# Later inverse products for the first head pair and earlier weight splits at the start, in a hybrid decoder layer on one Trainium2 core

## The chip, the cores and the metric

The kernel runs on one core of one Trainium2 chip. It is one program that computes a whole layer. The metric is the time of one execution on the device in microseconds (us); several runs are made and their median is given.

Engine names are those of the profile: PE is TensorE (matmuls and transposes; PEld is its weight load), DVE is VectorE, ACT is ScalarE, POOL is GpSimd, and SP is SyncE, which issues the DMAs. Each engine takes its instructions in its own fixed order; an instruction that waits holds up all behind it on the same engine.

## The reference

One layer on x of 512 positions by 1024 features in float32. It projects the normed x to eleven pieces; two token mixers work on them, a short gated convolution and a gated delta rule with 8 heads of 128; a sigmoid-gated sum of both, a residual add and a gated convolutional FFN follow.

```python
h = rmsnorm(x, norm_mix_g[l])
proj = h @ w_in[l]
bg, cg, xv, q, k, v, z, a, b, ga, gb = jnp.split(proj, pts, axis=-1)
y_a = short_conv_branch(bg, cg, xv, conv_a_w[l]) @ w_a_out[l]
y_b = gdn_branch(q, k, v, z, a, b, gdn_conv_w[l], gdn_A_log[l], gdn_dt_bias[l],
                 gdn_norm_g[l]) @ w_b_out[l]
mix = jax.nn.sigmoid(ga) * y_a + jax.nn.sigmoid(gb) * y_b
x = x + mix @ w_o[l]
h = rmsnorm(x, norm_ffn_g[l])
x = x + conv_ffn(h, w_up[l], ffn_conv_w[l], w_down[l])
```

Inside `gdn_branch` the sequence is cut into chunks. Each chunk needs the solution of a lower triangular system, and the chunks are then scanned in order:

```python
L = jnp.where(strict, jnp.einsum('bnhid,bnhjd->bnhij', k_beta, k) * decay, 0.0)
sol = lax.linalg.triangular_solve(eye + L, rhs, left_side=True, lower=True)
def step(state, inp):
    q_c, k_c, u_c, w_c, A_c, gl = inp
    v_new = u_c - jnp.einsum('bhcd,bhde->bhce', w_c, state)
    o = jnp.einsum('bhcd,bhde->bhce', q_c, state) + jnp.einsum('bhij,bhje->bhie', A_c, v_new)
    state = state * jnp.exp(gl)[..., None] + jnp.einsum('bhcd,bhce->bhde', k_c, v_new)
    return state, o
```

## The kernel before, in words

**Products.** A float32 product is made of three products of rounded operands: every weight and every activation is split into a high part (`wh`, `hT[0]`) and a low part (`wl`, `hT[1]`), and `mm3` (L114) adds low by high, high by low and high by high. The weights come in blocks of 1 MB (`raw`, two buffers, loaded at L133 on SP). A block is split in four quarters: ACT casts to `wh` (L138), DVE subtracts to `wl` (L139). The products of a block with hT are matmuls of 512 columns at L106.

**Jobs.** `run_jobs` (L181) goes through a list of blocks: k, q, v and z of head pair 0, of pair 1, k, q, v of pairs 2 and 3, z of both, then the gates, the convolution branch, the output weights and the FFN. At the start of job i the load of block i+2 is issued, and block i+1 is split while job i's products run.

**The order of the rest.** All other work is written as generators in queues (`backs`, `mids`, `chains`, `evacs`, `splits`, `sums_of`). After every slab, 4 matmuls of 512 columns (`SLAB`), `tick()` (L93) takes each queue one step further. So what is emitted between which products is set by how many bare `yield`s stand in a generator.

**A head pair** (two heads by four pieces of 128 positions, 8 matrices of 128x128) goes through three generators.

- `front(pr)` (L611) is in `chains`. It turns k and q (L608), makes products of k with k and q (L643), U and A from them, and the decay matrices Dm (exponentials on ACT, L525, one pair ahead). It inverts the 16x16 diagonal blocks by a recursion on DVE: U's blocks go through DRAM (`ucd`) to UB, 28 small instructions (L690, L692) make TB. TB goes back through DRAM (`tbd`, stored at L698) to T by four loads (L703) on SP.
- `mid(pr)` (L707) is in `mids`. It first waits `Y_T` = 17 slabs, then builds the whole inverse out of T: a DVE transpose TT (L711), products L718 and L727 of 32x32, L749, L760 and L763, L774, L780, with copies between them on ACT (L737, L753, L765, L767, L775, L781), DVE and POOL (L740). They end in `TTf`, which all pairs share.
- `back(pr)` (L786) is appended to `backs` when `mid` is done. It is the scan of four steps n with two heads: products L803 and L804 with the state, r on DVE (L806), the product L816 with TTf, vn on DVE (L818), products L825 (new state, L830 on DVE) and L836 (output, added on DVE at L840, squared on ACT at L841). At the end a factor `fac` (DVE L846, POOL L847) scales vs (L855), which is turned (L608) and multiplied into yb (L860).

The k job of pair 2 forces `back(0)` to its end (`reach`, L881), and so on for later pairs.

**The start** (L389 to L502). x comes in four tiles of 128 positions. For each, `norm_x(t)` squares it on ACT (L439) and makes the factor rt on DVE and POOL; `scale_x(t)` makes xr on DVE (L450); `turn_x` transposes it on PE (L455); `out_x` writes hT on ACT (L465) and DVE. Products with the first half of the positions (tiles 0 and 1) begin before the second half is there: those for the gates (`ab2`, 32 matmul rows) and those of K's first block. Its four quarters are split by four `ks.step()`, and DVE, ACT and POOL keep the order in which this part is written (`manual_schedule`, L471).

Of the kernel before, what the change touches and what calls it, by code (L numbers as in the profile page):

```python
# [28 lines left out]
Y_V, Y_T, Y_G, Y_N, Y_E, SLAB = 4, 17, 16, 3, 4, 4  # L29
Y_F = (5,4,4,2)  # L30
WARM = 3
WQ = 12


class Task:
# [23 lines left out]
def layer_kernel(ctx, tc, x, norm_mix_g, w_in, w_ab, conv_a_w, gdn_conv_w, gdn_A_log, gdn_dt_bias,  # L59
# [14 lines left out]
    def nm(s):  # L74
        cnt[0] += 1
        return f"{s}{cnt[0]}"
# [46 lines left out]
    class Block:  # L123
# [11 lines left out]
        def part(self, name, src):  # L135
            wh = self.wh[name] = wp.tile([P, *self.quarter], F32R, tag="wh", bufs=WQ, name=nm("wh"))
            wl = self.wl[name] = wp.tile([P, *self.quarter], F32R, tag="wl", bufs=WQ, name=nm("wl"))
            act.copy(out=wh, in_=src)  # L138
            dve.tensor_tensor(out=wl, in0=src, in1=wh.bitcast(F32), op=ALU.subtract)  # L139
# [211 lines left out]
    def ab_split():  # L351
        raw = ab_raw
        act.copy(out=ab2[:, :, 0:16], in_=raw)
        dve.tensor_tensor(out=ab2[:, :, 16:32], in0=raw, in1=ab2[:, :, 0:16].bitcast(F32), op=ALU.subtract)
# [34 lines left out]
    with tc.tile_pool(name="st1", bufs=1) as st1:  # L389
# [44 lines left out]
        def norm_x(t):  # L434
            sq = st1.tile([P, D], F32, tag="sq", bufs=2, name=nm("sq"))
            parts = halves[:1] if t > 1 else halves[1:]
            for i, sl in enumerate(parts):
                acc = sst[:, 2 * t + i:2 * t + i + 1]
                act.activation(out=sq[:, sl], in_=xts[t][:, sl], func=AF.Square, accum_out=acc)  # L439
                if i:  # L440
                    dve.scalar_tensor_tensor(out=rt[:, t:t + 1], in0=acc, scalar=1.0 / D, in1=rt[:, t:t + 1],
                                             op0=ALU.mult, op1=ALU.add)
                else:
                    dve.tensor_scalar(rt[:, t:t + 1], acc, 1.0 / D, EPS, op0=ALU.mult, op1=ALU.add)
            pool.tensor_tensor(out=rt[:, t:t + 1], in0=rt[:, t:t + 1], in1=nhalf[:, 0:1], op=ALU.pow)

        def scale_x(t):
            xr = xrs[t] = st1.tile([P, D], F32, tag="xr", bufs=2, name=nm("xr"))
            for sl in halves[:1] if t > 1 else halves[1:]:
                dve.tensor_scalar(xr[:, sl], xts[t][:, sl], rt[:, t:t + 1], None, op0=ALU.mult)  # L450

        def turn_x(t, bs):
            for k in range(ND):
                c = (k % 2) * HS + (t % 2) * P
                pe.transpose(out=bs[k // 2][:, c:c + P], in_=xrs[t][:, k * P:(k + 1) * P], identity=ident)  # L455

        def out_x(lo, bs):
            for ks in ((0, 2, 4, 6), (1, 3, 5, 7)):
                for lw in range(2):
                    for k in ks:  # L460
                        g = wA[:, 120 + k:121 + k]
                        src = bs[k // 2][:, (k % 2) * HS:(k % 2 + 1) * HS]
                        hh = hT[0][:, k, lo:lo + HS]
                        if lw == 0:
                            act.activation(out=hh, in_=src, func=AF.Copy, scale=g)  # L465
                        else:
                            dve.scalar_tensor_tensor(out=hT[1][:, k, lo:lo + HS], in0=src, scalar=g,
                                                     in1=hh.bitcast(F32), op0=ALU.mult, op1=ALU.subtract)

        bs = [bank() for _ in range(ND // 2)]  # L470
        with tc.manual_schedule(engines={mybir.EngineType.DVE, mybir.EngineType.Activation, mybir.EngineType.Pool}):  # L471
            pe.transpose(out=po[:, 0:P], in_=wr, identity=ident)
            norm_x(0)
            scale_x(0)
            turn_x(0, bs)
            norm_x(1)
            dve.tensor_copy(out=wA, in_=po[:, 0:P])
            scale_x(1)
            turn_x(1, bs)
            ab_split()  # L480
            out_x(0, bs)
            o_ab, o_k = bank(), [bank(), bank()]
            ab_products(o_ab, 0, HS)
            ks = Task(k_block.split())
            norm_x(2)
            ks.step()
            scale_x(2)
            norm_x(3)
            ks.step()
            scale_x(3)  # L490
            ks.finish()
            constants()
            products(o_k[0], k_block.wh, k_block.wl, 0, hT, 0, HS, range(ND))
            bs = [bank() for _ in range(ND // 2)]
            for t in (2, 3):
                turn_x(t, bs)
            out_x(HS, bs)
            products(o_k[1], k_block.wh, k_block.wl, 1, hT, 0, HS, range(ND))
# [206 lines left out]
        mids.append(mtask[pr])  # L705

    def mid(pr, U, um, T, rest):  # L707
        for _ in range(Y_T):
            yield
        TT = tl("TT", 2, (P, 8, 32))  # L710
        dve.transpose(out=flat(TT), in_=flat(T))  # L711
        yield
        yield
        o = bank()
        for f in range(8):
            for q in range(4):
                sl = slice(32 * q, 32 * q + 32)
                pe.matmul(o[sl, 32 * f:32 * f + 32], lhsT=um[sl, f, :], rhs=T[sl, f, :], start=True, stop=True)  # L718
        Y = tl("Y", 2, (P, 8, 32))
        act.copy(out=flat(Y), in_=o[:, 0:256])  # L720
        yield
        yield
        o = bank()
        for f in range(8):
            for q in range(4):
                sl = slice(32 * q, 32 * q + 32)
                pe.matmul(o[sl, 32 * f:32 * f + 32], lhsT=TT[sl, f, :], rhs=Y[sl, f, :], start=True, stop=True)  # L727
        T2 = tl("T", 2, (P, 8, 32))
        dve.tensor_tensor(out=flat(T2), in0=flat(T), in1=o[:, 0:256], op=ALU.subtract)
        T = T2  # L730
        TT = tl("TT", 2, (P, 8, 32))
        dve.transpose(out=flat(TT), in_=flat(T))
        reach(pr - 1, SCANNED)
        for q in range(4):
            sl = slice(32 * q, 32 * q + 32)
            if q < 2:
                act.copy(out=T64[sl, :, sl], in_=T[sl])  # L737
        for q in (2, 3, 0, 1):
            sl = slice(32 * q, 32 * q + 32)
            pool.tensor_copy(out=TTf[sl, :, sl], in_=TT[sl])  # L740
        yield
        yield
        s0, s1 = slice(0, 32), slice(32, 64)
        qa = [slice(64 * b, 64 * b + 32) for b in range(2)]
        qb = [slice(64 * b + 32, 64 * b + 64) for b in range(2)]
        o = bank()
        for f in range(8):
            for b in range(2):
                pe.matmul(o[qb[b], 32 * f:32 * f + 32], lhsT=U[qa[b], f, qb[b]], rhs=T[qa[b], f, :],  # L749
                          start=True, stop=True)  # L750
        Y = tl("Y", 2, (P, 8, 32))
        for b in range(2):
            act.copy(out=flat(Y[qb[b]]), in_=o[qb[b], 0:256])  # L753
        yield
        yield
        o1, o2 = bank(), bank()
        for f in range(8):
            fs = slice(32 * f, 32 * f + 32)
            for b in range(2):
                pe.matmul(o1[qa[b], fs], lhsT=Y[qb[b], f, :], rhs=TT[qb[b], f, :], start=True, stop=True)  # L760
        for f in range(8):
            fs = slice(32 * f, 32 * f + 32)
            pe.matmul(o2[s1, fs], lhsT=TT[s1, f, :], rhs=Y[s1, f, :], start=True, stop=True)  # L763
        v32 = lambda a: a.rearrange("p (f c) -> p f c", c=32)
        act.activation(out=T64[s1, :, s0], in_=v32(o2[s1, 0:256]), func=AF.Copy, scale=-1.0)  # L765
        for b in (1, 0):
            act.activation(out=TTf[qa[b], :, qb[b]], in_=v32(o1[qa[b], 0:256]), func=AF.Copy, scale=-1.0)  # L767
        yield
        yield
        Y64 = tl("Y64", 1, (P, 8, 64))  # L770
        lo, hi = slice(0, 64), slice(64, 128)
        o = bank()
        for f in range(8):
            pe.matmul(o[hi, 64 * f:64 * f + 64], lhsT=U[lo, f, hi], rhs=T64[:, f, :], start=True, stop=True)  # L774
        act.copy(out=flat(Y64[hi]), in_=o[hi, :])  # L775
        yield
        yield
        o1 = bank()
        for f in range(8):
            pe.matmul(o1[lo, 64 * f:64 * f + 64], lhsT=Y64[hi, f, :], rhs=TTf[hi, f, hi], start=True, stop=True)  # L780
        act.activation(out=TTf[lo, :, hi], in_=o1[lo, :].rearrange("p (f c) -> p f c", c=64),  # L781
                       func=AF.Copy, scale=-1.0)
        ctask[pr] = Task(back(*rest))
        backs.append(ctask[pr])
# [543 lines left out]
```

## Time and profile before

| | us |
|---|---|
| median of 3 runs | 998.35 |
| lowest, highest run | 998.03, 1000.19 |
| the profiled execution | 1001.66 |
| span of the profile | 1000.0 |
| mean granted TensorE clock in it | 0.99 |
| stretch of pair 0 from the last product ahead of L718 to the end of the inverse, and some products behind it | 94.38 to 126.58 |
| the like stretch of pair 1 | 168.58 to 191.08 |

The span runs from the first to the last instruction of the profiled execution; a little of its time lies outside. In the rows that are quoted below, a row of the timeline gives the start and the length in us, engine, line, operation, tiles written and read, how many instructions of the kind follow one another (x4), and in brackets how long the engine was idle before and what ended that. Matmuls overlap, so starts tell more of PE than ends.

### The profile page before, as it was taken

To read this page: it belongs to the slowest core of one execution; us is meant where nothing else is said; L and a number is where in the kernel's file an instruction comes from. 1 tells how busy PE (TensorE), PEld (TensorE's weight loads), DVE (VectorE), ACT (ScalarE), POOL (GpSimd) and SP (SyncE) were. 2 spreads that over 40 slices of the span, in tenths; PEclk is the share of its full clock that TensorE was granted. 3 is DMA by queue.
4 is the path that set the end of the run, shared out by engine and by line. 5 is a ranking of instruction groups with operands and counts; after the bars stand their busy time and mean duration, and the time that the engine had idled before them with its cause. 6 is when DMAs were issued, how large, how long until landed. Compare 5 with 4: busy or idle time off the path is not lost.

```text
span 1000.0 us, 15801 instructions
## 1 busy us (share of the span) xinstructions
PE 981.1 (98%) x6250; PEld 847.1 (85%) x6250; DVE 677.0 (68%) x1312; ACT 470.4 (47%) x1023; POOL 60.3 (6%) x101
## 2 busy tenths in 40 slices
PE   8998999999999999999999999999999999999997
PEld 5886788887878889999988888998899988888886
DVE  5868378687634867799953552899888888643325
ACT  6785374666434434344742222555454556322313
POOL 3320120202010000000000000000000000000000
PEclk9999799999999999999999999999999999999999
DMA  6443023223121212322432243212323224233202
GB/s 222 144 135 109 27 71 94 75 82 100 53 85 44 85 48 82 124 86 85 169 126 85 91 158 151 104 45 85 126 90 122 85 85 168 85 99 112 85 1 84
DMA packets 33467, 97.71 MB, mean 98 GB/s; under 512 B 19276, under 2 KB 19697, under 8 KB 23025
## 3 DMA queue, kind: packets, MB, share of 16 engines
q1 hardware_dynamic: 33392, 96.70, 28.9%
q8 instruction: 49, 0.80, 0.3%
q14 instruction: 26, 0.20, 0.1%
HBM read 93.27 MB, written 3.42 MB: 97 GB/s over the span
## 4 chain that ended last, share of the span: by engine, by line
PE 95%; DVE 2%; issue 1%; DMA 1%; ACT 1%; SPq 0%; POOL 0%; POOLq 0%; DVEq 0%; ACTq 0%
PE ps L106 86%; PE ps L608 1%; PE ps L643 1%; DMA xt<-in_x_dram 1%; PE ps L816 1%; PE ps L836 1%; DVE cv L304 1%; PE ps L825 1%; PE ps L804 1%; PE ps L803 1%; PE ps L774 0%; PE ps L780 0%; DVE wl L139 0%; PE ps L1150 0%; PE ps L727 0%
## 5 line engine op out<-in xcount | busy, mean ns | idle before, releaser
L138 ACT CAST wh<-raw 128x512 fp32r<-128x512 f32 x378 | 222.2, 618 | 284.7 <-PE ps L106 245.2
L139 DVE TENSOR_TENSOR wl<-raw,wh 128x512 fp32r<-128x512 f32 x378 | 252.2, 687 | 135.3 <-ACT wh L138 134.0
L106 PE MATMUL ps<-hT,wh 128*128 128x512 f32 (+1 forms) x1104 | 320.5, 371 | 1.8 <-ACT wh L138 1.8
L106 PEld LDWEIGHTS ps<-hT,wh 128*128 128x128 f32 x1104 | 198.5, 191 | 30.4 <-ACT wh L138 2.1
L106 PE MATMUL ps<-hT,wl 128*128 128x512 f32 (+1 forms) x552 | 197.6, 367 | 0.9 <-issue 0.5
L106 PE MATMUL ps<-h,wh 128*128 128x512 f32 (+1 forms) x704 | 177.9, 342 | 0.0
L106 PEld LDWEIGHTS ps<-h,wh 128*128 128x128 f32 x704 | 122.6, 190 | 15.0
L106 PEld LDWEIGHTS ps<-hT,wl 128*128 128x128 f32 x552 | 106.2, 192 | 15.8 <-issue 1.3
L106 PE MATMUL ps<-h,wl 128*128 128x512 f32 (+1 forms) x352 | 114.6, 341 | 0.0
L106 PE MATMUL ps<-wh,as 128*128 128x512 f32 x352 | 108.6, 389 | 0.0
L106 PEld LDWEIGHTS ps<-wh,as 128*128 128x128 f32 x352 | 66.1, 188 | 13.6
L106 PEld LDWEIGHTS ps<-h,wl 128*128 128x128 f32 x352 | 66.8, 190 | 7.6
L106 PE MATMUL ps<-wl,as 128*128 128x512 f32 x176 | 68.5, 389 | 0.0
L106 PE MATMUL ps<-ts,wh 128*128 128x256 f32 x320 | 59.2, 283 | 0.0
L304 DVE SCALAR_TENSOR_TENSOR cv<-ps,wA,cv 128x511 f32<-128x511 f32 (+2 forms) x72 | 53.2, 739 | 4.7 <-ACT cv L301 4.4
L106 PEld LDWEIGHTS ps<-ts,wh 128*128 128x128 f32 x320 | 50.6, 192 | 0.0
L159 DVE TENSOR_TENSOR raw<-raw 128x512 f32<-128x512 f32 x72 | 49.4, 686 | 0.9
L106 PE MATMUL ps<-us,wh 128*128 128x256 f32 x256 | 47.4, 283 | 0.0
L106 PEld LDWEIGHTS ps<-us,wh 128*128 128x128 f32 x256 | 40.5, 192 | 0.0
L106 PE MATMUL ps<-wh,mix 128*128 128x512 f32 x128 | 40.2, 391 | 0.0
L106 PE MATMUL ps<-ts,wl 128*128 128x256 f32 x160 | 40.1, 283 | 0.0
L106 PE MATMUL ps<-yb,wh 128*128 128x512 f32 x128 | 39.6, 389 | 0.0
(260 smaller groups left out, 1305.9 us busy)
## 6 DMA issues: line engine op xcount, KB each, us to landing
raw<-in_w_in_dram SPq DMA_DIRECT2D x36, 1024.0 KB, 4.9
raw<-in_w_up_dram SPq DMA_DIRECT2D x22, 1024.0 KB, 4.8
raw<-in_w_down_dram SPq DMA_DIRECT2D x11, 1024.0 KB, 4.9
raw<-in_w_a_out_dram SPq DMA_DIRECT2D x4, 1024.0 KB, 5.0
raw<-in_w_b_out_dram SPq DMA_DIRECT2D x4, 1024.0 KB, 5.0
raw<-in_w_o_dram SPq DMA_DIRECT2D x4, 1024.0 KB, 4.9
Dm<-gtd SPq DMA_DIRECT2D x4, 512.0 KB, 3.9
x<-in_x_dram SPq DMA_DIRECT2D x4, 512.0 KB, 6.4
```

The source lines that it names most:

```text
L106: pe.matmul(o, lhsT=a, rhs=b, start=start, stop=stop, skip_group_check=free)
L138: act.copy(out=wh, in_=src)
L139: dve.tensor_tensor(out=wl, in0=src, in1=wh.bitcast(F32), op=ALU.subtract)
L159: dve.tensor_tensor(out=r[q], in0=a, in1=b, op=op)
L304: dve.scalar_tensor_tensor(out=dst[:, sh:], in0=src[:, :S - sh], scalar=wcol(j), in1=dst[:, sh:], op0=ALU.mult, op1=ALU.add)
L608: pe.transpose(out=o[:, n * P:(n + 1) * P], in_=src[:, n * P:(n + 1) * P], identity=ident)
L643: pe.matmul(o[:, i], lhsT=kqs[:, a, h, 0, sl], rhs=kqs[:, b, h, :, sl], start=a > 0, stop=a + b == 0)
L803: pe.matmul(o[:, 0:P], lhsT=kq[:, h, 0, sl], rhs=St[h], start=True, stop=True)
L804: pe.matmul(o[:, P:2 * P], lhsT=kq[:, h, 1, sl], rhs=St[h], start=True, stop=True)
L816: pe.matmul(o[:, 0:P], lhsT=TTf[:, f, :], rhs=rs[h], start=True, stop=True)
L825: pe.matmul(o2[:, 0:P], lhsT=kn[:, f, :], rhs=vns[h], start=True, stop=True)
L836: pe.matmul(o[:, 0:P], lhsT=A[:, f, :], rhs=vns[h], start=True, stop=True)
```

## The change

Two edits. `mid` of pair 0 waits `Y_T + Y_M` = 27 slabs ahead of its first step where it waited 17; the other pairs wait 17 as before. And in the start the first two `ks.step()`, which split the first two quarters of K's first block, stand ahead of `norm_x(2)`; one stood behind it and one behind `norm_x(3)`. No instruction is added or taken out. All lines behind L32 have a number higher by one in the changed kernel.

```diff
 WQ = 12
+Y_M = 10
@@
             ks = Task(k_block.split())
+            ks.step()
+            ks.step()
             norm_x(2)
-            ks.step()
             scale_x(2)
             norm_x(3)
-            ks.step()
             scale_x(3)
             ks.finish()
@@
     def mid(pr, U, um, T, rest):
-        for _ in range(Y_T):
+        for _ in range(Y_T if pr else Y_T + Y_M):
             yield
```

ACT at the start, where `sq` is the square of a tile of x (L439, then L440) and `wh` a cast of a weight quarter. Before:

```order
L465 ACTIVATE hT_80<-ps_152,wA 128x256
L439 ACTIVATE sq_228,sst<-xt_130 128x1024
L138 CAST wh_232<-raw_128 128x512
L439 ACTIVATE sq_238,sst<-xt_132 128x1024
L138 CAST wh_242<-raw_128 128x512
L138 CAST wh_248<-raw_128 128x512
L138 CAST wh_252<-raw_128 128x512
```

In the changed kernel:

```order
L466 ACTIVATE hT_80<-ps_152,wA 128x256
L139 CAST wh_228<-raw_128 128x512
L139 CAST wh_232<-raw_128 128x512
L440 ACTIVATE sq_236,sst<-xt_130 128x1024
L440 ACTIVATE sq_242,sst<-xt_132 128x1024
L139 CAST wh_248<-raw_128 128x512
L139 CAST wh_252<-raw_128 128x512
```

Both casts that PE's first products of K need now stand ahead of the squares of the third and fourth tile. DVE's subtractions move in the same way.

PE at the first inverse product of pair 0 (L718, then L719, which reads T and um). Before:

```order
L106 MATMUL ps_1078<-hT_80,wh_980 128x512 x2
L106 MATMUL ps_1078<-hT_80,wh_972 128x512 x2
L718 MATMUL ps_1105<-T_959,um_779 32x32 x32
L727 MATMUL ps_1148<-Y_1138,TT_1091 32x32 x32
L106 MATMUL ps_1193<-hT_81,wh_1038 128x512
```

In the changed kernel:

```order
L107 MATMUL ps_1186<-hT_80,wl_1059 128x512
L107 MATMUL ps_1186<-hT_81,wh_1058 128x512
L107 MATMUL ps_1186<-hT_80,wl_1059 128x512
L719 MATMUL ps_1204<-T_959,um_779 32x32 x32
L644 MATMUL ps_1243<-kqs_1007 128x256 x6
L107 MATMUL ps_1186<-hT_81,wh_1066 128x512
```

Between the products `ps_1078`, after which L718 stood, and the new place lie 32 matmuls of 512 columns and two groups of four transposes of pair 1's k (L609). L727 no longer follows L718 at once, and pair 1's products of k and q (L643, then L644) stand between the steps of pair 0's inverse.

DVE in the scan of pair 0 (r, vn: L806 and L818, then one higher; sub and TB: the recursion of pair 1). Before:

```order
L806 SCALAR_TENSOR_TENSOR r_1523<-ps_1520,neG,vs_802 128x128
L806 SCALAR_TENSOR_TENSOR r_1529<-ps_1526,neG,vs_802 128x128
L304 SCALAR_TENSOR_TENSOR cv_1508<-ps_1324,wA,cv_1508 128x509
L818 TENSOR_SCALAR vn_1553<-ps_1551,ap_665 128x128
L818 TENSOR_SCALAR vn_1557<-ps_1555,ap_665 128x128
```

In the changed kernel:

```order
L807 SCALAR_TENSOR_TENSOR r_1555<-ps_1552,neG,vs_802 128x128
L691 TENSOR_TENSOR sub_1579<-UB_1365,TB_1366 64x50
L807 SCALAR_TENSOR_TENSOR r_1561<-ps_1558,neG,vs_802 128x128
L693 TENSOR_TENSOR TB_1366<-TB_1366,sub_1579 64x10x5
L691 TENSOR_TENSOR sub_1579<-UB_1365,TB_1366 64x54
L693 TENSOR_TENSOR TB_1366<-TB_1366,sub_1579 64x9x6
L691 TENSOR_TENSOR sub_1579<-UB_1365,TB_1366 64x56
L819 TENSOR_SCALAR vn_1571<-ps_1569,ap_665 128x128
L819 TENSOR_SCALAR vn_1575<-ps_1573,ap_665 128x128
```

The recursion of pair 1, which came behind the scan of pair 0, now runs among its steps, since the scan starts ten slabs later and the recursion does not.

## The prediction

> **What bounds the kernel now.** I read first the page's head, its busy times and the slices of the TensorE clock, then the table of waits of PE, then windows over the places that these name.
>
> ```profile
> span 1000.0 us, 15801 instructions
> PE 981.1 (98%) x6250; PEld 847.1 (85%) x6250; DVE 677.0 (68%) x1312; ACT 470.4 (47%) x1023; POOL 60.3 (6%) x101
> PEclk9999799999999999999999999999999999999999
> ...
> PE ps L718 <- DMA T<-tbd: 3.6, 4, 2.7
> PE ps L727 <- DVE TT L711: 2.1, 1, 2.1
> PE ps L106 <- ACT wh L138: 1.8, 1, 1.8
> ```
>
> PE is busy for 98% of the span, so only two things can be won: PE's few waits, and time in which its clock was low. The fifth slice (100 to 125 us) has a clock of 0.7. The three longest waits after the first load (in us: total, times, longest) are those that the change touches. In the windows below (start:end, length, busy time of PE, PEld, DVE, ACT, POOL, granted clock, DMA share, GB/s) both stand out again.
>
> ```profile
> 10.46:13.87 3.41, 2.71 (x14) 1.38 (x14) 2.43 (x7) 2.00 (x6) 0.00 (x0) 1.00 0.71 205
> 13.87:17.28 3.41, 1.64 (x11) 1.44 (x12) 2.01 (x5) 3.41 (x8) 1.05 (x3) 1.00 0.68 283
> 17.28:20.70 3.42, 3.42 (x18) 3.42 (x17) 2.21 (x4) 0.57 (x2) 2.99 (x11) 0.50 0.13 17
> 94.38:126.58 32.20, 25.97 (x323) 20.63 (x324) 14.32 (x33) 13.40 (x42) 3.22 (x5) 0.79 0.13 38
> 168.58:191.08 22.50, 22.50 (x332) 18.62 (x332) 14.47 (x33) 14.24 (x43) 3.71 (x5) 1.00 0.15 49
> 99.20:112.86 13.66, 11.01 (x164) 7.82 (x153) 1.91 (x4) 2.76 (x7) 1.57 (x4) 0.50 0.17 69
> ```
>
> A low clock comes in steps of 3.4 us: 3.42 us after a window in which PE was idle for 3.41 - 1.64 = 1.77 us, and 13.66 = 4 x 3.415 us after the waits at L718 and L727. An idle of 3.41 - 2.71 = 0.70 us (first row) cut nothing: the next window ran at 1.00. One such window costs 3.42 x (1 - 0.5) = 1.7 us if PE has work for it.
>
> The Trainium skill (TensorE: Matmul & The Clock Gate, Part 1: The HAM clock gate) says that the clock halves after an idle window of about 3.4 us, 3413 ns on a free-running counter. The length agrees with the rows. That the window must be idle does not: PE worked for 1.64 us of the one that cut. The measurement decides; what the page's rule would make of the new waits is the first rival.
>
> **Removed: the stall at the first inverse.**
>
> ```profile
> 92.40 1.98 PE L106 MATMUL ps<-hT,wh 128*128 128x512 f32 x8
> 95.18 1.78 SPq L703 DMA_DIRECT2D T<-tbd  x4
> 98.61 0.69 PE L718 MATMUL ps<-T,um 32*32 32x32 f32 x58 [0.24 <-DMA T<-tbd]
> ...
> 157.61 2.20 PE L106 MATMUL ps<-hT,wh 128*128 128x512 f32 x9
> 159.65 0.39 PE L106 MATMUL ps<-hT,wl 128*128 128x512 f32 x1
> ```
>
> In the timeline (start, us, engine, line, operation) PE runs out at 92.40 + 1.98 = 94.38. The four loads of T are issued only at 95.18; the last T is there at 98.61. In the order of the change the first L718 stands behind 32 more products of 512 columns, each (159.65 - 157.61) / 9 = 0.227 us: 7.3 us. PE comes to it at 94.38 + 7.3 = 101.7, without counting two groups of transposes, and T has been there for 3 us; TT (L711) too, on a DVE that is less than half busy there. So both waits go, and with them the four low windows.
>
> What that is worth I take from pair 1, whose same stretch runs from L718 to the end of its inverse without a wait: 22.50 us at clock 1.00. It has the eight 512-column products more that the change of place put there (8 x 0.227 = 1.8), so pair 0's stretch would be 20.7 in its place, and the loss is 32.2 - 20.7 = **11.5 us**. As a check: waits 3.6 + 2.1 + four windows of 1.7 = 12.5. I keep 11.5, bounds 10.5 to 12.5.
>
> **Moved: the splits of K's first weights.**
>
> ```profile
> 4.31 0.43 SPq L133 DMA_DIRECT2D raw<-in_w_in_dram  x1
> raw<-in_w_in_dram SPq DMA_DIRECT2D x1, 1024.0 KB, 7.8
> ...
> 9.16 3.02 ACT L465 ACTIVATE hT<-ps,wA 128x256 fp32r<-128x256 f32 x8 [1.48 <-PE ps L455]
> 13.59 1.06 ACT L439 ACTIVATE sq<-xt 128x1024 f32<-128x1024 f32 x1 [1.41 <-DMA xt<-in_x_dram]
> 14.64 0.60 ACT L138 CAST wh<-raw 128x512 fp32r<-128x512 f32 x1
> 15.15 1.05 ACT L439 ACTIVATE sq<-xt 128x1024 f32<-128x1024 f32 x1
> 17.45 0.75 DVE L450 TENSOR_SCALAR xr<-xt,rt 128x1024 f32<-128x1024 f32 x1
> 9.69 3.79 PE L106 MATMUL ps<-hT,ab 128*32 128x256 f32 x16
> 15.30 0.38 PE L106 MATMUL ps<-hT,wh 128*128 128x256 f32 x1 [1.82 <-ACT wh L138]
> 25.13 2.02 PE L106 MATMUL ps<-hT,ab 128*32 128x256 f32 x16
> 26.98 0.28 PE L106 MATMUL ps<-hT,wh 128*128 128x256 f32 x1
> ```
>
> ACT is free at 9.16 + 3.02 = 12.18 and waits to 13.59 for tile 3 of x, with the cast behind it in its queue. The raw weights landed at 4.31 + 7.8 = 12.1. So two casts of 0.60 fit into ACT's wait (12.2 to 13.4), and PE, free at 9.69 + 3.79 = 13.48, goes on at once: 1.82 us won. The idle of the window 13.87 to 17.28 falls under the 0.70 that cut nothing, so its 1.7 us of low clock goes too. Late next is the fourth tile. Its square now starts at 13.59 + 1.06 and its xr is done some 3.05 us behind that square's start (17.45 + 0.75 - 15.15), at 17.7, about 18 behind the two subtractions now ahead on DVE. PE has till then 24 products of (26.98 - 25.13) / 16 = 0.116 us, 2.8, and eight transposes, 1.0: it runs out at 17.3 and waits 0.7. Start-up: 1.82 + 1.7 - 0.7 = **2.8 us**; bounds 1.1 (one window is cut by the new wait after all) and 3.5 (no new wait).
>
> **Added: waits where pair 0's inverse and scan now stand.** The scan is now emitted among pair 1's turn, L643 products and TB recursion. No row shows this mixture; each price is bounded by the nearest rows.
>
> ```profile
> 135.27 0.60 PE L816 MATMUL ps<-r,TTf 128*128 128x128 f32 x4
> 135.69 0.61 DVE L818 TENSOR_SCALAR vn<-ps,ap 128x128 f32<-128x128 f32 x2 [0.58 <-PE ps L816]
> 137.07 0.60 DVE L830 SCALAR_TENSOR_TENSOR S<-S,eGl,ps 128x128 f32<-128x128 f32 x2
> 137.59 0.48 DVE L840 TENSOR_TENSOR vs<-vs,ps 128x128 f32<-128x128 f32 x2
> 139.11 0.80 DVE L806 SCALAR_TENSOR_TENSOR r<-ps,neG,vs 128x128 f32<-128x128 f32 x2 [1.04 <-PE ps L804]
> 140.28 0.61 PE L816 MATMUL ps<-r,TTf 128*128 128x128 f32 x4
> 141.65 0.60 PE L836 MATMUL ps<-vn,A 128*128 128x128 f32 x4
> 145.57 0.29 DVE L855 TENSOR_SCALAR vs<-vs,fac 128x128 f32<-128x128 f32 x1 [1.43 <-POOL fac L847]
> ...
> 150.46 0.21 DVE L690 TENSOR_TENSOR sub<-UB,TB 64x56 f32<-64x56 f32 x1
> 150.70 0.21 DVE L692 TENSOR_TENSOR TB<-TB,sub 64x56 f32<-64x56 f32 x1
> ...
> 206.17 0.60 PE L836 MATMUL ps<-vn,A 128*128 128x128 f32 x4
> 211.49 0.33 PE L608 MATMUL ps<-ident,vs 128*128 128x128 f32 x1 [0.81 <-DVE vs L855]
> ```
>
> Inverse: the copies of T and TTf now share ACT with pair 1's squares and casts. I take 0.3, between nothing (pair 1's inverse has no wait) and the dearest such wait, 2.1.
>
> Scan: a step takes PE 140.28 - 135.27 = 5.0 us. DVE's own part of it is 0.61 + 0.60 + 0.48 + 0.80 = 2.5 us; about twelve recursion steps of 150.70 - 150.46 = 0.24 now stand between, 2.9. That makes 5.4 against 5.0, 0.4 a step over four steps: 1.6. Queued behind a late L818 are L830 and L840 on DVE, and PE's next L825 waits for it. Bounds: nothing, and one recursion pair (0.48) ahead of each of eight handovers, 3.8. The exponentials of pair 2, with the table load ahead of them, now come on ACT in mid-scan; the upper bound holds what they hold up.
>
> Output turn: the first L608 on vs now stands 12 products, 2.7 us, behind the last L836. The way from that L836 to the scaled vs took 145.57 - 141.65 = 3.9 us with DVE nearly clear, and 211.49 - 206.17 = 5.3 in pair 1. I take 5.3, since two subtractions now stand in it as there: 5.3 - 2.7 = 2.6. Bounds: 3.9 - 2.7 = 1.2, and 4.0 with two more instructions of 0.7 ahead.
>
> Clock: an idle of 2.6 us is more than the 1.77 that cut, so one window, 1.7. Bounds: nothing, and two windows, 3.4.
>
> Added together 0.3 + 1.6 + 2.6 + 1.7 = **6.2 us**, between 1.2 and 13.3.
>
> At nothing I cost SP's loads (the round trip of T and the raw blocks change places, each with microseconds to spare) and POOL's (6% busy).
>
> **The sum.** 11.5 + 2.8 - 6.2 = 8.1 us less. The profiled execution took 1001.66 us, span 1000.0, so it would take 993.5. It lies 3.3 us above the median of 998.35. Some of that may be a longer stall at L718 in this one execution, which I cannot see in the others; I count half of it, 1.65, as not to be won there. Beside the median the change then wins 11.5 + 2.8 - 1.65 = 12.65 and pays 6.2: 998.35 - 12.65 + 6.2 = 991.9, so **992 us**. On this change alone 988.5 to 996.
>
> **The rivals.**
>
> *The clock holds through the new waits.* If only a window with hardly any work cuts, the wait of 2.6 us, spread over two windows or beside 0.8 us of work in one, leaves the clock at 1.00. For it: the window with 0.70 us of idle. Against it: the one with 1.77 and 1.64 of work. It gives 1.7 less, 990.2. The Trainium skill (TensorE: Matmul & The Clock Gate, Part 1: The HAM clock gate) has this rule.
>
> *The new waits are hidden.* Pair 1's own scan, beside pair 2's front, has one wait of 0.8 us in this trace. Then about 1.5 of the 6.2 comes: 998.35 - 12.65 + 1.5 = 987.2. Against it: the recursion of the next pair and the twelve products are not what pair 1 has.
>
> *The stall is only moved.* The waits come near their upper bounds, 2.1 + 3.8 + 4.0 and two windows of 1.7, 13.3 in all: 998.35 - 12.65 + 13.3 = 999.0. Against it: it needs every handover late.
>
> *Slower: a low clock across the scan.* If PE idles for over 1.8 us early in the scan, the clock drops there; at half clock each link of the scan takes longer, and the idles between keep it low, as they did for four windows behind L718. Held over four steps and the turn, some 23 us, that is seven windows, 7 x 1.7 = 11.9, with the waits of 0.3 + 1.6 + 2.6 = 4.5 it is 16.4: 998.35 - 12.65 + 16.4 = 1002.1. From six windows on it is slower by more than can be told from no change. Against it: a slow PE waits less for the others, and four windows in a row stood behind 3.6 + 2.1 = 5.7 us of waits at once.
>
> *The change does not do what it says.* T still missing at L718 is shut out by 3 us. That the raw weights land behind the third tile would lose the 2.8 us: 994.7; they are issued ahead of it and landed 1.5 us earlier.
>
> **How the numbers follow.** The forecast 0.56, the clock holding 0.15, hidden waits 0.12, only moved 0.08, slower 0.06, weights late 0.03. The range for 8 in 10 cuts off a little at the hidden waits and takes in most of the forecast's worse half: 987 to 997. What a measurement of this kernel can tell from no change is about 0.2%, 2.0 us. Faster by more (under 996.35) are all of the clock holding, the hidden waits and late weights, and 0.52 of the forecast: 0.82. Within it: the forecast's other 0.04 and 0.06 of the moved stall, 0.10. Slower: 0.08.
>
> **What would show it.** In the changed kernel's trace: no wait at the first L719 and clock 1.00 from 94 to 113; no wait at L107 near 13.5 and 1.00 from 17.3 to 20.7; waits of 1.2 to 4 us at the L609 on vs of pair 0, with one low window behind; small waits at L817 or L826. A low clock for over six windows in the scan, or a wait for T again, would make the prediction wrong.

## The result, and the profile after

| | before | changed |
|---|---|---|
| median of 4 runs, us | 998.19 | 988.01 |
| lowest, highest | 995.16, 1000.19 | 987.75, 989.34 |
| span of the profiled execution | 1000.0 | 986.0 |

The ratio is 0.9903 with a 95% interval of 0.9876 to 0.993: 10 us or 1% faster. The forecast was 992 in a range of 987 to 997. The time lies in the range, but below the forecast's own 988.5 to 996, next to the second rival (the new waits are hidden, 987.2).

The head of the changed kernel's page, and the longest waits of PE (us in total, times, longest):

```profile
span 986.0 us, 15803 instructions
PE 974.4 (99%) x6250; PEld 841.9 (85%) x6250; DVE 677.1 (69%) x1312; ACT 470.3 (48%) x1023; POOL 60.6 (6%) x101
PEclk9999999999999999999999999999999999999999
...
PE ps L609 <- DVE vs L856: 2.0, 3, 0.8
PE ps L430 <- DVE warm L394: 1.5, 1, 1.5
PE ps L728 <- DVE U L648: 0.5, 1, 0.5
PE ps L456 <- DVE xr L451: 0.4, 1, 0.4
```

The waits for T, for TT and for the first cast of K are gone, and so is the 7 in the clock's row. New is the wait at L609 for the scaled vs; 0.8 of its 2.0 us is pair 1's, which stood before too. The windows of the changed kernel (start:end, length, busy time of PE, PEld, DVE, ACT, POOL, clock, DMA share, GB/s):

```profile
10.46:13.87 3.41, 3.11 (x19) 1.92 (x19) 3.41 (x8) 3.41 (x9) 0.00 (x0) 1.00 0.99 326
13.87:17.28 3.41, 3.41 (x31) 3.20 (x29) 1.87 (x6) 2.42 (x6) 1.90 (x4) 1.00 0.56 228
17.28:20.70 3.42, 3.34 (x27) 3.14 (x28) 3.42 (x8) 2.97 (x9) 2.90 (x12) 1.00 0.30 72
94.00:114.00 20.00, 20.00 (x301) 16.18 (x300) 14.51 (x33) 13.50 (x49) 7.23 (x9) 1.00 0.37 96
139.22:142.63 3.41, 2.25 (x11) 1.45 (x10) 2.89 (x8) 0.17 (x1) 0.49 (x1) 1.00 0.65 269
```

In the start the window that had 1.77 us of idle is full, and from 94 to 114 us PE does not stop. Of these rows only the last, at the output turn, has an idle of note, 1.16 us, and the clock stayed.

To see where the time came from, I counted the products of 512 columns that read hT and a weight (L106, then L107) in the timelines. There are 2880 of them, in the same order in all kernels. The table compares the starts of the 1st, the 240th (the last one ahead of the old place of L718), the 391st (past pair 0's turn) and the last.

| us | before | changed | gain |
|---|---|---|---|
| start to 1st | 33.29 | 29.66 | 3.63 |
| 1st to 240th | 60.70 | 60.71 | 0 |
| 240th to 391st | 66.79 | 56.81 | 9.98 |
| 391st to last | 832.33 | 832.02 | 0.31 |

So all but 0.3 us of the 14 us between the two profiled executions lies in the two places of the change.

### The profile page after: what moved, and what is told of

The parts are those of the page before. It is cut to its first block, busy times and chain, and to the rows that moved or that the text cites. A ratio compares the mean times of both kernels' runs of the same rounds, so it can differ in the third digit from the quotient of the medians.

```text
span 986.0 us, 15803 instructions
## 1 busy us (share of the span) xinstructions
PE 974.4 (99%) x6250; PEld 841.9 (85%) x6250; DVE 677.1 (69%) x1312; ACT 470.3 (48%) x1023; POOL 60.6 (6%) x101
## 3 DMA queue, kind: packets, MB, share of 16 engines
q1 hardware_dynamic: 33392, 96.70, 29.5%
HBM read 93.27 MB, written 3.42 MB: 98 GB/s over the span
## 4 chain that ended last, share of the span: by engine, by line
PE 94%; DVE 2%; ACT 2%; issue 1%; POOL 1%; DMA 0%; SPq 0%; POOLq 0%; DVEq 0%
PE ps L107 86%; PE ps L609 1%; PE ps L644 1%; PE ps L817 1%; PE ps L837 0%; PE ps L826 0%; PE ps L781 0%; PE ps L775 0%; PE ps L805 0%; PE ps L804 0%; DMA xt<-in_x_dram 0%; PE ps L1151 0%; POOL fac L848 0%; DVE wl L140 0%; ACT hT L466 0%
## 5 line engine op out<-in xcount | busy, mean ns | idle before, releaser
L107 PE MATMUL ps<-hT,wh 128*128 128x512 f32 (+1 forms) x1104 | 318.1, 368 | 0.0
L107 PEld LDWEIGHTS ps<-hT,wh 128*128 128x128 f32 x1104 | 196.2, 189 | 27.9
L107 PE MATMUL ps<-hT,wl 128*128 128x512 f32 (+1 forms) x552 | 194.7, 362 | 0.1
L107 PE MATMUL ps<-h,wh 128*128 128x512 f32 (+1 forms) x704 | 177.9, 341 | 0.0
L107 PEld LDWEIGHTS ps<-h,wh 128*128 128x128 f32 x704 | 122.5, 189 | 15.0
L107 PEld LDWEIGHTS ps<-hT,wl 128*128 128x128 f32 x552 | 104.5, 189 | 14.2 <-DVE wl L140 0.5
L107 PE MATMUL ps<-h,wl 128*128 128x512 f32 (+1 forms) x352 | 114.6, 341 | 0.0
L107 PE MATMUL ps<-wh,as 128*128 128x512 f32 x352 | 108.4, 389 | 0.0
L107 PEld LDWEIGHTS ps<-wh,as 128*128 128x128 f32 x352 | 66.1, 188 | 13.7
L107 PEld LDWEIGHTS ps<-h,wl 128*128 128x128 f32 x352 | 66.7, 190 | 7.6
L107 PE MATMUL ps<-wl,as 128*128 128x512 f32 x176 | 68.5, 389 | 0.0
L107 PE MATMUL ps<-ts,wh 128*128 128x256 f32 x320 | 59.2, 283 | 0.0
L305 DVE SCALAR_TENSOR_TENSOR cv<-ps,wA,cv 128x511 f32<-128x511 f32 (+2 forms) x72 | 53.2, 740 | 3.2 <-ACT cv L302 2.9
L107 PEld LDWEIGHTS ps<-ts,wh 128*128 128x128 f32 x320 | 50.6, 192 | 0.0
L107 PE MATMUL ps<-us,wh 128*128 128x256 f32 x256 | 47.4, 283 | 0.0
L107 PEld LDWEIGHTS ps<-us,wh 128*128 128x128 f32 x256 | 40.5, 192 | 0.0
L107 PE MATMUL ps<-ts,wl 128*128 128x256 f32 x160 | 40.1, 283 | 0.0
L107 PE MATMUL ps<-wh,mix 128*128 128x512 f32 x128 | 40.1, 391 | 0.0
L107 PE MATMUL ps<-yas,wh 128*128 128x512 f32 x128 | 39.6, 389 | 0.0
```

The lines of the kernel that those rows point to most:

```text
L107: pe.matmul(o, lhsT=a, rhs=b, start=start, stop=stop, skip_group_check=free)
L305: dve.scalar_tensor_tensor(out=dst[:, sh:], in0=src[:, :S - sh], scalar=wcol(j), in1=dst[:, sh:], op0=ALU.mult, op1=ALU.add)
```

## The experiments

The measure for the second place is the stretch from the 240th to the 391st product. In every kernel PE has the same work in it: 515 matmuls and transposes, equal in number line by line. It is 55.2 us in the three executions in which PE did not wait at all in it (e4, e10, e11 below), so what is over 55.2 is counted here as waits and low clock. The compared kernel is the one before, run on the same chip; its medians there were 996.92 (e1 to e4), 998.26 (e5 to e8) and 997.6 (e9 to e11).

**One part alone.** e1 keeps `Y_M = 0` and moves only the splits; e2 moves only the inverse:

```diff
-Y_M = 10
+Y_M = 0
```

> Only the earlier splits of K's first two quarters; the inverse of pair 0 stands where it stood before. Theory A (the two edits act apart from each other, each in its own stretch): the wait of 2.2 us at the first product of K (1.82 and 0.34 us) and one low clock window (1.7 us) go, so the second gates product starts 3.6 to 3.9 us earlier than in the kernel before (21.3 to 21.5 us in place of 25.1), and the stall at the first inverse product stays, 10 to 12.5 us. Span some 996.3, median 3.5 us under before. Theory B (the start gained 3.6 us in the changed kernel because the third tile of x happened to land 0.7 us earlier in that execution): the fourth tile is waited for by about 0.7 us and the gain is 2.8 to 2.9.

Measured: 994.74 us, ratio 0.9982 (0.9971 to 0.9994). The second gates product started at 21.71 and the 1st wide product at 29.90, 3.4 us earlier than before, and PE did not wait for the fourth tile. That is nearer to theory A, but it does not rule out theory B: in e1, too, the third tile was there early, by 13.13 us, when its square started without a wait. The stall was there, but cheaper than expected: the stretch took 63.82 us, 8.6 over 55.2 where the kernel before had 66.79 - 55.2 = 11.6. The waits and windows of e1:

```profile
PE ps L719 <- DMA T<-tbd: 3.3, 4, 2.6
PE ps L728 <- DVE TT L712: 2.4, 1, 2.4
...
89.14:92.55 3.41, 1.84 (x9) 1.18 (x7) 2.15 (x4) 2.31 (x5) 0.00 (x0) 1.00 0.47 130
92.55:95.96 3.41, 1.34 (x64) 1.02 (x64) 2.83 (x5) 0.90 (x2) 0.00 (x0) 1.00 0.55 96
95.96:99.38 3.42, 1.37 (x65) 1.33 (x66) 1.28 (x3) 1.06 (x3) 0.00 (x0) 0.50 0.62 256
99.38:102.79 3.41, 3.12 (x7) 1.96 (x7) 0.63 (x2) 0.81 (x2) 1.57 (x4) 0.50 0.02 5
102.79:106.20 3.41, 3.41 (x66) 2.40 (x66) 0.00 (x0) 0.73 (x2) 0.00 (x0) 1.00 0.00 0
```

and the windows of the kernel before at the same place:

```profile
95.80:99.22 3.42, 1.26 (x64) 1.02 (x64) 2.98 (x5) 0.91 (x3) 0.00 (x0) 1.00 0.53 86
99.22:102.63 3.41, 1.30 (x73) 1.19 (x66) 1.13 (x3) 1.21 (x3) 0.00 (x0) 0.50 0.66 267
102.63:106.04 3.41, 2.87 (x6) 1.78 (x7) 0.78 (x2) 0.81 (x2) 1.57 (x4) 0.50 0.02 5
106.04:109.46 3.42, 3.42 (x38) 2.42 (x37) 0.00 (x0) 0.73 (x2) 0.00 (x0) 0.50 0.00 0
109.46:112.87 3.41, 3.41 (x46) 2.44 (x45) 0.00 (x0) 0.01 (x1) 0.00 (x0) 0.50 0.00 0
```

The waits add up to the same (5.7 us in both), but two windows ran low in e1 and four before. So the same waits cost 3 us more or less, two windows of 1.7. Why two windows more stayed low in one of the two executions is not shown here; the last two of them had PE at work throughout.

For e2 the first part goes back, against the changed kernel:

```diff
-            ks.step()
-            ks.step()
             norm_x(2)
+            ks.step()
             scale_x(2)
             norm_x(3)
+            ks.step()
             scale_x(3)
```

> Only the later inverse of pair 0; the start is as before. Theory A: the wait at the first product of K (2.2 us) and the low window from 17 to 21 us are there, the stall at the first inverse product (11.5 us) is not, and the output turn of pair 0 waits 1.2 us: 11.5 - 1.2 = 10.3 us less than the profile before, span some 989.7, and clock 1.00 from 92 to 116 us. Theory B (the clock stays full in the stretch of the inverse only because nothing was low earlier, or the new waits are only hidden when everything comes 3.6 us earlier): a low window or waits of over 2 us come back in the scan, and less than 8 us is won.

Measured: 990.42 us, ratio 0.9934 (0.9919 to 0.9949), span 988.9. The stretch took 56.78 us, as in the changed kernel (56.81): in these executions the second place owes nothing to the first. In the start PE waited 1.2 and 0.3 us, less than the expected 2.2, and one window was low. Theory A. Of the medians, e1 wins 2.2 and e2 6.5 us, together 8.7, against 10.0 to 10.2 for both; the kernel before alone varies by 5 us from run to run, so the 1.4 us between are not to be read as an effect.

**Is the scan bounded by DVE?** The changed kernel with the recursion's product made three times:

```diff
-            dve.tensor_tensor(out=t, in0=UB[:, j, j + 1:16]...
+            for _ in range(3 if pr == 1 else 1):
+                dve.tensor_tensor(out=t, in0=UB[:, j, j + 1:16]...
```

> The changed kernel, with the product of each step of pair 1's recursion (L691) made three times in place of once, same result: 28 more instructions of some 0.24 us on DVE, 6.7 us, most of them among the scan of pair 0. Theory A (the scan's hand-overs are covered by the products between them, and DVE has room there): under 1.5 us of new waits on PE. Theory B (the step of the scan is bounded by DVE, 5.4 us of DVE to 5.0 of PE as the prediction reckoned): each of some two and a half steps grows by 2.9 us, 5 to 7 us longer than the changed kernel, span 991 to 993.

Measured: 986.98 us (986.86 to 989.01), span 987.3; the stretch took 56.13 us, no longer than the changed kernel's 56.81. (The profiled execution was the slowest of the four, 989.01; its 1st wide product started at 31.50.) Theory A. The only wait that names the recursion is one of 0.9 us at the turn. A step of the scan in the changed kernel, and then two in e3 (columns as in the windows above):

```profile
124.90:129.91 5.01, 5.01 (x34) 4.49 (x33) 4.49 (x23) 2.42 (x8) 0.00 (x0) 1.00 0.00 0
```

```profile
126.75:131.75 5.00, 5.00 (x33) 4.49 (x32) 4.60 (x22) 2.37 (x8) 0.00 (x0) 1.00 0.00 0
131.75:136.76 5.01, 5.01 (x33) 4.49 (x32) 4.66 (x23) 4.98 (x17) 0.00 (x0) 1.00 0.00 2
```

A step takes 5.0 us with PE never idle, in all three. The tripled recursion does not crowd a step further: in the order of DVE's instructions it spreads over more steps (still running at the turn), with DVE at 4.6 to 4.7 of 5.0 us. So more work on DVE cost the scan nothing, but no step held more than DVE can do in 5.0 us; what such a step would cost is not shown.

**What the turn waits for.** With `Y_M = 8` 20 products stand between pair 0's last L837 and its turn, with 10 there are 12, with 14 there are 11:

```diff
-Y_M = 10
+Y_M = 8
```

> The changed kernel with 8 slabs more in place of 10. The first inverse product stands 24 products of 512 columns (5.5 us and two groups of transposes) behind the old place in place of 32, T was there 4.2 us behind it; the output turn of pair 0 stands 20 products (4.5 us) behind the last L837 in place of 12 (2.7 us). Theory A (the only new wait is the way from L837 to the scaled vs, 3.5 to 3.9 us, against the products that cover it): no wait at T, none or up to 0.3 us at the first turn, span 0.8 to 1.2 us under the changed kernel's, some 985. Theory B (the waits at the turn come from DVE being busy with the convolution of the next k, whatever stands in front): the 1.2 us stay, span 986.

Measured: 986.82 us (986.5 to 987.06), span 985.3. No wait at pair 0's turn; the stretch took 55.22 us, 1.6 less than with 10 slabs. Theory A. A wait of 0.6 us appeared in pair 1's inverse (L728, ACT's copy of Y), which gives some of it back. For 14 slabs:

> The changed kernel with 14 slabs more. The end of pair 0's scan is now forced by the k job of pair 2: 3 products between the last L817 and L837, 11 ahead of the first turn. Theory A (each new wait is the chain's length less the products that cover it): 0.3 to 0.7 us at L837, the turn's waits of 1.2 us grow by up to 0.5, span 986.3 to 987.2. Theory B (my prediction's size, a crowded scan pays several us and a low window): span 990 or more.

Measured: 987.65 us (987.58 to 987.71), span 985.9, stretch 56.62: one wait of 1.13 us at the turn, none at L837. That is far from theory B. Of theory A the waits it asked for did not come: nothing at L837, and the turn waited 1.13 us in place of 1.2 to 1.7.

**How long a wait halves the clock.** Three kernels leave waits of other lengths: 2 slabs and 6 slabs in place of 10, and one split in place of two ahead of the third tile's square.

> The changed kernel with 2 slabs more in place of 10. PE now reaches the bulk of the first inverse products 5 products (1.1 us) behind the old place, T landed 4.2 us behind it, and L728 stands 3 products behind them. Both theories: 2.5 to 3 us of waiting for T, about 1.4 us (2.1 less 0.7) at L728, no wait at the output turn of pair 0, so 2.8 us more waiting than in the changed kernel. Theory A (an idle of about 1.8 us in one window of 3.4 us halves the clock for the next): at least two low windows, 3.4 us more, span 991 to 993. Theory B (only a window with hardly any work halves it): clock 1.00, span 988 to 989.

Measured: 993.46 us, ratio 0.9962 (0.9949 to 0.9974), span 991.5, stretch 61.52: 6.3 over 55.2, of it 2.8 a wait for T and 3.4 two low windows. The expected wait at L728 did not come. The low windows are theory A's; but the window ahead of them had only 0.68 us of work, so that this run alone does not rule out theory B.

> The changed kernel with 6 slabs more. T is there (24 products behind the old place), but L728 stands right behind L719 with nothing between, as in the kernel before; the output turn stands 28 products behind the last L837. Both theories: no wait for T, 2.1 to 2.7 us at L728 (ACT's copy of Y), none at the turn: 1 us more waiting than the changed kernel. Theory A (1.8 us of idle in one window halves the clock): 1.7 us more if the wait falls within one window, span 987 to 989. Theory B: clock 1.00, span 986.5 to 987.2.

Measured: 987.96 us, span 986.0, stretch 56.91, one wait of 1.2 us at L728, clock 1.00. The wait came out at half of what both theories asked for, so it does not tell them apart.

```diff
             ks.step()
-            ks.step()
             norm_x(2)
             scale_x(2)
             norm_x(3)
+            ks.step()
             scale_x(3)
```

> The changed kernel with only the first quarter of K split ahead of the third tile's square; the second again behind the fourth tile's. PE starts the products of K at once, and after eight of them (0.9 us) waits for the second quarter: cast behind both squares, at some 15.9 us with the third tile landing at 13.6 (15.2 with 12.9), so 1 to 1.7 us of wait in place of none. Theory A (over 1.8 us of idle in one window is needed to halve the clock): no low window, the start 0.9 to 1.7 us longer than in the changed kernel, second gates product at 22.4 to 23.2. Theory B (any wait over 1 us halves it): 1.7 us more, 24 to 25.

Measured: 988.85 us (988.27 to 990.8), span 989.1; the profiled execution was the slowest of the four. In it PE waited 2.0 us up to 16.36, more than expected: the third tile's transposes stood next on PE, and their xr was done at 16.21, the second quarter's cast not much later. One window was low; the 1st wide product started at 32.73, 3.1 later than in the changed kernel. With 2.0 us of idle both theories have the low window, so this too leaves the choice open; but with one split ahead most of the start's gain was lost in this execution. One window of each kernel that bears on the question, in the order e5, e6, e8 and e2, each with the window behind it:

```profile
90.77:94.19 3.42, 0.68 (x3) 0.22 (x2) 2.30 (x4) 2.70 (x5) 0.00 (x0) 1.00 0.30 37
94.19:97.60 3.41, 3.38 (x11) 1.82 (x11) 1.97 (x4) 1.25 (x2) 0.00 (x0) 0.50 0.72 188
```

```profile
96.65:100.06 3.41, 2.23 (x118) 1.46 (x118) 2.56 (x5) 2.59 (x11) 0.00 (x0) 1.00 0.61 255
100.06:103.47 3.41, 3.41 (x77) 2.71 (x66) 3.10 (x6) 2.62 (x11) 0.70 (x2) 1.00 0.02 5
```

```profile
13.42:16.83 3.41, 1.41 (x12) 1.23 (x12) 1.37 (x4) 3.24 (x7) 1.02 (x2) 1.00 0.71 286
16.83:20.24 3.41, 3.41 (x19) 3.41 (x18) 2.25 (x4) 0.61 (x2) 2.98 (x11) 0.50 0.18 24
```

```profile
12.38:15.80 3.42, 1.86 (x13) 1.35 (x12) 1.81 (x5) 3.01 (x6) 0.55 (x1) 1.00 0.94 331
15.80:19.21 3.41, 3.41 (x18) 3.41 (x17) 2.75 (x6) 1.25 (x3) 2.96 (x8) 0.50 0.02 7
```

Idle of 2.74, 2.00 and 1.56 us halved the clock of the next window; 1.18 did not, nor 1.57 in e1's window from 89.14, nor 1.42 in that of the kernel before from 92.39. In e2 PE worked for 1.86 us of the window, more than half: that rules out theory B. Between 11 us and the last 20 us of the thirteen profiled executions every window at full clock with an idle of 1.77 us or more was followed by a low one, and none with 1.42 or less. So the border lies between these, near 1.6 us or 45% of a window. Since 1.56 cut and 1.57 did not, the idle time alone, with the modelled ends of matmuls, does not fix it.

**The changed kernel again, and a better one.** e9 is the changed kernel, e10 has 8 slabs, and e11 has 8 slabs and pair 1's inverse three slabs earlier:

```diff
-        for _ in range(Y_T if pr else Y_T + Y_M):
+        for _ in range(Y_T + Y_M if pr == 0 else Y_T - (pr == 1) * 3):
```

> The changed kernel as it is, beside the next two on one chip. Expected: median 987 to 989, output turn of pair 0 with 1.2 us of waits, clock 1.00 from 10 us to the last 6 us.

> 8 slabs in place of 10, once more beside the changed kernel. Theory A (the turn's wait is the way to the scaled vs less the products ahead of it, and 20 products cover it): the stretch from the last product ahead of the old place to 150 products later is 1.2 to 1.6 us shorter than in the changed kernel, median about 1 us lower. Theory B (the gap between e4 and the changed kernel was the start of one execution): same median within 0.5 us and the same stretch.

> 8 slabs for pair 0, and pair 1's inverse three slabs earlier (14 in place of 17), so that pair 1's output turn stands 16 products (3.6 us) behind its last L837 in place of 13. Theory A: the wait of 0.8 us at that turn goes, T of pair 1 is there in time (landed 6 to 7 us ahead), span 0.6 to 1.0 us under that of 8 slabs alone. Theory B (the turn waits for DVE's other work, not for the chain): no difference.

| | median of 5, us | lowest, highest | ratio to before (95%) | stretch |
|---|---|---|---|---|
| e9, 10 slabs | 987.56 | 987.33, 987.65 | 0.9905 (0.9887 to 0.9923) | 56.77 |
| e10, 8 slabs | 986.97 | 986.66, 987.25 | 0.9899 (0.9882 to 0.9917) | 55.25 |
| e11, 8 slabs, pair 1 at 14 | 985.32 | 984.63, 985.81 | 0.9882 (0.9862 to 0.9902) | 55.22 |

e9 came as expected, with 1.17 us of waits at the turn of pair 0. For e10 theory A: the stretch is 1.5 us shorter again, and the median 0.6 lower, since the 0.6 us at pair 1's L728 came again. For e11 theory A: pair 1's wait at the turn is gone, and the one at L728 too, so that more is won than the expected 0.6 to 1.0; a wait of 0.4 us for pair 1's T is new. The view of PE's waits lists only these:

```profile
PE ps L430 <- DVE warm L394: 1.5, 1, 1.5
PE ps L537 <- ACT abT L533: 0.4, 1, 0.4
PE ps L719 <- DMA T<-tbd: 0.4, 1, 0.4
```

e11 beats both kernels: 985.32 against 987.56 and 997.6 on the same chip, and its slowest run is faster than the fastest run of the changed kernel.

## Why the prediction came out as it did

**The stall at the first inverse (11.5 us): right.** The stretch had 66.79 - 55.2 = 11.6 us over a stretch without waits, and T was never waited for at the new place. What the estimate could not see is that this is one execution's price: in e1 it was 8.6. The prediction took half of the profile's 3.3 us over the median off the gain; the size fits the two windows, 3.4 us, by which the two profiled stalls differ. The spread of the kernel before (994.6 to 1000.2 over all its runs, against 987.3 to 989.3 for the changed one) fits this too, for the granted clock of its runs is on record: the 35 runs beside the experiments took 994.6 to 996.1 us where it was 0.995, and 999.8 to 1000.1 where it was 0.990. A difference of 0.005 in some 997 us is 5.0 us. So the spread is time at the low clock; at which place in the kernel it lay is known for the profiled executions only.

**The start (2.8 us): right, but for the new wait's size.** The wait for the cast and the low window went, and with them a wait of 0.34 us at L106 that the sum had left out. The new wait of 0.7 us for the fourth tile did not come in this execution. The rows of the changed kernel show why:

```profile
11.87 1.19 ACT L139 CAST wh<-raw 128x512 fp32r<-128x512 f32 x2
12.90 1.13 ACT L440 ACTIVATE sq<-xt 128x1024 f32<-128x1024 f32 x1
...
16.24 2.10 PE L456 MATMUL ps<-ident,xr 128*128 128x128 f32 x16
21.50 2.02 PE L107 MATMUL ps<-hT,ab 128*32 128x256 f32 x16
```

The third tile was there by 12.90, 0.7 us before it was in the profile before (13.59). Where its square had to wait for it and started later (13.32 in e10, 13.82 in e3), PE did wait for the fourth tile, 0.3 us in both: the mechanism holds, with less than half of the price. Over the profiled executions the 1st wide product started at 30.0 on average with both splits ahead (ten executions, 29.5 to 31.5) and at 32.9 without (two, 32.5 and 33.3): 2.9 us. The arrival of the third tile varies by 1 us among them (12.79 to 13.82 where it was waited for), so that 2.9 lies so near to 2.8 partly by luck.

**The new waits (6.2 us): the step that failed, in size.** Against 55.2 the changed kernel's stretch has 1.6 us. Its parts:

- Inverse, 0.3: no wait.
- Scan, 1.6: no wait. The prediction added twelve recursion steps of 0.24 us to 2.5 us of the scan's own DVE work and got 5.4 of DVE to 5.0 of PE in each of four steps. Two things are wrong in this. The recursion has only 28 instructions, so twelve a step can stand in 2.3 steps and not in four; in the changed kernel they ran from 121.78 to 131.07, not quite two steps. And the measured step has 4.49 although some 15 of them fall into it: with 2.35 us for the scan's own eight instructions that leaves 0.14 us for each. The 0.24 us was the distance of two starts in a chain in which each instruction needs the one before. An instruction that does not need the one ahead of it starts sooner:

```profile
125.24 0.21 DVE L691 TENSOR_TENSOR sub<-UB,TB 64x56 f32<-64x56 f32 x1
125.37 0.59 DVE L819 TENSOR_SCALAR vn<-ps,ap 128x128 f32<-128x128 f32 x2
125.89 0.20 DVE L693 TENSOR_TENSOR TB<-TB,sub 64x56 f32<-64x56 f32 x1
```

The first vn starts 0.13 us behind the recursion's product, not 0.24, and ahead of that product's end. The kernel before showed the same where pair 0's scaling ran among pair 1's recursion: an L690 at 146.66, the L855 behind it at 146.77, 0.11 us later. A sum of distances along a chain bounds the chain, not the engine.

- Output turn, 2.6: measured 1.16 in two waits, at the lower bound of 1.2. The way from L837 to the scaled vs took 3.5 us, nearer to pair 0's own 3.9 before than to pair 1's 5.3, which I chose:

```profile
136.28 0.61 PE L837 MATMUL ps<-vn,A 128*128 128x128 f32 x4
139.74 0.88 DVE L856 TENSOR_SCALAR vs<-vs,fac 128x128 f32<-128x128 f32 x4 [1.76 <-POOL fac L848]
140.17 0.83 PE L609 MATMUL ps<-ident,vs 128*128 128x128 f32 x4 [0.55 <-DVE vs L856]
140.53 0.75 DVE L305 SCALAR_TENSOR_TENSOR cv<-ps,wA,cv 128x511 f32<-128x511 f32 x1
141.19 0.28 DVE L856 TENSOR_SCALAR vs<-vs,fac 128x128 f32<-128x128 f32 x1
141.62 0.30 PE L609 MATMUL ps<-ident,vs 128*128 128x128 f32 x1 [0.61 <-DVE vs L856]
```

  DVE is idle for 1.76 us ahead of the first scaling: POOL's instruction, not DVE's queue, sets this way, and the first wait, 0.55 us, is the way less its cover. The second, 0.61, is another: here DVE's queue sets it, for an instruction of the next k's convolution (L305, 0.75 us) stands between the fourth scaling and the fifth. In e4, with 20 products in place of 12, all eight scalings ran together from 138.59 on (1.66 us), and both waits went:

```profile
140.11 1.03 PE L609 MATMUL ps<-ident,vs 128*128 128x128 f32 x8
```

  Of the stretch's 1.6 us the remaining 0.45 shows as no wait; what it is stays open.
- Clock, 1.7: no low window. It hung on the wait of 2.6; the 1.16 us that came stay under what halved it elsewhere.

So of the rivals the hidden waits came nearest, with 1.6 for its 1.5 us. Its chance of 0.12 looks too low: four small prices were each taken above the lower bound that the nearest quiet row gave, and all four came out at that bound. The first rival (the clock holds through a wait of 2.6 us) cannot be judged by the changed kernel, since that wait did not come. The Trainium skill (TensorE: Matmul & The Clock Gate, Part 1: The HAM clock gate) asks for an idle window to halve the clock. The traces differ: 1.56 us of idle in a window of 3.42 did it (e2), and 2.00 (e8), so its rule would price such waits too low. The stall that only moves and the low clock across the scan did not come, and no run here brought them about.

## What to carry to other kernels

Price a stall by two lines, the wait and the low clock windows behind it, and compare the stretch with a like one that has no wait: the windows doubled the price here (5.7 us of waits, 11.6 in all), and made it differ by 3 us between two executions. When work is moved under cover, count the products that stand between the ends of the chain that was moved: 12 products (2.7 us) against a way of 3.5 left a wait, 20 left none. And do not add up distances of a dependent chain as load on its engine: among other work an instruction of the chain took about 0.14 us of DVE here, not 0.24. Count the instructions first, too; 28 cannot load four steps with twelve each.

## What the runs showed of the hardware that was not expected

The clock was halved after windows in which PE still worked for more than half of the time (1.86 of 3.42 us, e2). The way back is not even either. In the kernel before the window from 106.04 to 109.46 was full and the next was low all the same, and in e5 the one from 94.19 with 3.38 us of work was followed by a second low one. In the starts of the kernel before, e2 and e8 one full low window was enough, and in e1 one with 3.12 us of work (99.38 to 102.79). What tells these apart was not tried.
